# Phase 1 of a one-core transformer layer: the adaLN dot products in two passes, none on GpSimd, and the row modulation on ScalarE

## The chip, the cores and the metric

The kernel runs on one core of a Trainium2 chip as one launch. The metric is device time in microseconds (us) of that launch, the median of a few runs. The five engines of the core have one instruction queue each and run it in order: TensorE (PE in the profile; its weight loads are PEld), VectorE (DVE), ScalarE (ACT), GpSimd (POOL) and SyncE (SP). In this kernel SP issues every DMA transfer that the program asks for.

## The reference, cut to what matters

One layer for 2048 latent tokens and a prompt of 128 context tokens, both through the same weights, width 1024. Each of the two token kinds has its own conditioning vector: `c` for the latents, `c_ctx` for the prompt.

```python
def modulation(cond, w_ada, b_ada):
    m = jax.nn.silu(cond) @ w_ada + b_ada          # (1024) @ (1024, 6144)
    return jnp.split(m, 6, axis=-1)                # shift, scale, gate; twice
...
    u = rms_norm(x, g_pre) * (1.0 + scale) + shift
    p = u @ w_in                                   # q, k, v, B, C, x_in
```

Behind that come differential attention with a softmax over 2176 keys, a gated convolution, the output projection, and a SwiGLU feed-forward part with hidden width 2816; the second half of the layer is modulated in the same way by the remaining columns of `m`. Outputs are the two token sets and the keys and values of the prompt.

## The kernel before, in words

All matrix products of weights are made in split form: an operand is held as a high part `h` and a remainder `l` (`split`, L79: ScalarE copies to `h`, VectorE or GpSimd subtracts for `l`), and three matmuls replace one.

**Phase 1** (the stretch that the change touches) makes q, k and v of all tokens. Tokens go in nine groups: group 0 to 7 are 256 latent tokens each (two row tiles of 128), group 8 is the prompt (one tile). For a group, `norm_rows` (L193) loads rows `xt`, takes the sum of squares on ScalarE and scales by the reciprocal root on GpSimd; `u_part` (L211) transposes two of the eight 128-column blocks at a time on TensorE into the PSUM tile `up`, modulates them into `ut` (L223), splits them into `uh` and `ul`, and stores both in DRAM (`ud`) for later phases. `qkv_group` (L367) multiplies, rotates q and k, transposes them and stores them.

**The modulation** itself has no matmul. The host has cut `w_ada` into 48 blocks of 128 output columns, each transposed to 128x1024 (512 KB). Block b is loaded as `raw`, and the dot product of each of its rows with a conditioning vector, which lies in all partitions in `cb`, gives one column of `mc`: on VectorE one instruction with a sum (L138), on GpSimd a product `prod` (L142) that ScalarE then sums (L143). `ada_cols` (L145, instructions L148 to L150) makes shift and scale columns `modc` of that. Blocks 0 to 15 are shift and scale of the first half of the layer, blocks 2 kt and 2 kt + 1 those of column block kt; 16 to 31 are those of the second half; 32 to 47 are the gates.

**The start.** Group 0 runs along with the loading: for each kt from 0 to 7, `ada_first(kt)` loads two blocks and takes the dot products with both conditioning vectors (with `c` at raised priority), `qkv_weights(kt, (0, 1))` loads and splits the q and k weights of that kt (the remainders `wl` on GpSimd), and `follow` issues the twelve matmuls of that kt. The v weights follow (remainders on VectorE), then v of group 0. There are 6 `raw` buffers and 3 `rawq` buffers in the start, and 4 `raw` buffers later.

**Behind the start** the groups run in the order 0, 1, 2, 8, 3, 4, 5, 6, 7. While a group is multiplied, the rows and `u_part` of the next are made, and blocks 16 to 47 are worked off four per group (`ada_steps`), each with both dot products.

The order of instructions on each engine is not the order of the code alone: the build schedules them by a simulated timeline, with `tc.high_priority` raising some and `tc.issue_after` holding DMAs behind a named instruction. Phases 2 (attention, the convolution branch, output projection) and 3 (feed-forward) follow in the same launch.

Of the kernel before, what the change touches and what calls it, by code (L numbers as in the profile page):

```python
# [8 lines left out]
F32 = mybir.dt.float32  # L9
F32R = mybir.dt.float32r  # L10
BF16 = mybir.dt.bfloat16
AF = mybir.ActivationFunctionType
ALU = mybir.AluOpType
# [4 lines left out]
P = 128  # L18
D = 1024
# [13 lines left out]

POOLW = 960
WLV = (2,)
RAWS, FIRST = 6, "VG"
RATE = (670, 1500)


# [1 line left out]
def layer(ctx, tc, x_prompt, x_sample, cache_k, cache_v, cond, w_ada, b_ada, gcol,  # L41
# [81 lines left out]
    def cond_load(c):  # L123
        dma(cb[:, c, :], cond[c].partition_broadcast(P))
        S.activation(cb[:, c, :], cb[:, c, :], AF.Silu)

    first = {}

    def ada_load(b):
        raw = ad.tile([P, D], F32, tag="raw", name="raw", bufs=RAWS if b < 16 else 4)  # L130
        first[b] = dma(raw, w_ada[b])
        return raw

    def ada_sum(b, raw, c, eng):

        if eng is V:
            junk = cbp.tile([P, D], BF16, tag="jv", name="jv")
            V.scalar_tensor_tensor(junk, raw, 1.0, cb[:, c, :], op0=ALU.mult, op1=ALU.mult,  # L138
                                   accum_out=mc[:, b, c:c + 1])
        else:  # L140
            prod = cbp.tile([P, D], F32, tag="prod", name="prod", bufs=1)
            G.tensor_tensor(prod, raw, cb[:, c, :], op=ALU.mult)  # L142
            S.activation(prod, prod, AF.Copy, accum_out=mc[:, b, c:c + 1])  # L143

    def ada_cols(i, kt, cs):  # L145

# [3 lines left out]
        V.tensor_scalar(modc[:, i, cs, kt], modc[:, i, cs, kt], gc[:, i // 2, kt:kt + 1], None, op0=ALU.mult)  # L150

    def ada_first(kt):
        raws = [ada_load(2 * kt + j) for j in range(2)]
        with tc.high_priority(offset=400):
            for j in range(2):
                ada_sum(2 * kt + j, raws[j], 0, V)
            ada_cols(0, kt, slice(0, 1))
        if kt == 0:
            cond_load(1)
        for j in range(2):  # L160
            ada_sum(2 * kt + j, raws[j], 1, V if FIRST[j] == "V" else G)
        ada_cols(0, kt, slice(1, 2))

    def ada_later(b):
        raw = ada_load(b)
        ada_sum(b, raw, 0, V)
        ada_sum(b, raw, 1, V)
        if b < 32:
            if b % 2:
                ada_cols(2, (b - 16) // 2, slice(0, 2))  # L170
            return
        which, k = divmod(b - 32, KT)
        V.tensor_scalar(gates[:, which, :, k], mc[:, b, :], bc[:, b:b + 1], gc[:, 2 + which, k:k + 1],
                        op0=ALU.add, op1=ALU.mult)
        if b == 47:
            ps = psu.tile([P, 512], F32, tag="psu", name="gt")
            T.transpose(ps[:32, :P], gates.rearrange("p w c k -> p (w c k)"), ident)
            gt = p1.tile([32, P], F32, name="gt")
            S.copy(gt, ps[:32, :P])
            dma(ggd.rearrange("w (k n) -> (w k) n", n=P), gt)  # L180
# [29 lines left out]
    def u_part(xs, gi, kk, between=None):  # L210

        n, c = len(xs), int(gi == 8)
        w = n * P
        up = psu.tile([P, 512], F32, tag="psu", name="up")
        ut = p1.tile([P, 2, 256], F32, tag="ut", name="ut", bufs=2)
        h = p1.tile([P, 2, 256], F32R, tag="uh", name="uh", bufs=6)
        l = p1.tile([P, 2, 256], F32R, tag="ul", name="ul", bufs=6)
        for a in range(2):
            kt = 2 * kk + a
            for i in range(n):  # L220
                T.transpose(up[:, a * 256 + i * P:a * 256 + (i + 1) * P],
                            xs[i][:, kt * P:(kt + 1) * P], ident)
            V.tensor_scalar(ut[:, a, :w], up[:, a * 256:a * 256 + w],  # L223
                            modc[:, 0, c, kt:kt + 1], modc[:, 1, c, kt:kt + 1],
                            op0=ALU.mult, op1=ALU.add)
            if between:
                split(h[:, a, :w], l[:, a, :w], ut[:, a, :w])
                between(kt, h[:, a, :], l[:, a, :])
        if not between:
            split(h[:, :, :w], l[:, :, :w], ut[:, :, :w])  # L230
        dma(ud[gi][0, :, 2 * kk:2 * kk + 2, :w], h[:, :, :w])
        dma(ud[gi][1, :, 2 * kk:2 * kk + 2, :w], l[:, :, :w])
        return [(h[:, a, :], l[:, a, :]) for a in range(2)]
# [102 lines left out]
    for kk in range(4):  # L336
        u_part(xs, 0, kk, follow)
    behind.append(first[13])
    for kt in range(KT):
        qkv_weights(kt, (2,))  # L340
    x_ad.close()
# [91 lines left out]
            wb[m] = (h, l)  # L433

    order = [0, 1, 2, 8, 3, 4, 5, 6, 7]
    ada_work = list(range(16, 48))
    rows = {}
    for n, gi in enumerate(order):
        nxt = order[n + 1] if n < 8 else None

        def ada_steps(k):
            for b in ada_work[:k]:
                ada_later(b)
            del ada_work[:k]
# [6 lines left out]
        def part_step(a):  # L451
            if nxt is not None:
                u.setdefault(nxt, [])
                for kk in (0, 1) if a == 0 else (2, 3):
                    u[nxt] += u_part(rows[nxt], nxt, kk)
            ada_steps(1)

        steps = {1: rows_step, 0: lambda: part_step(0), 2: lambda: part_step(1)}
        if nxt is None:
# [424 lines left out]
    j = 0  # L884
# [275 lines left out]
```

## Time and profile before

| | |
|---|---|
| median of 3 runs | 3061.99 us (3058.2 to 3064.18) |
| the profiled execution's own time | 3067.98 us |
| its span, first to last instruction | 3066.2 us |
| busy in the span | PE 2909.8 us, DVE 1994.7 us, ACT 1444.4 us, POOL 1230.1 us |
| DMA | 525.25 MB, mean 171 GB/s |
| last matmul-like instruction of phase 1 on PE | starts at 406.6 us |
| first scores of phase 2 on PE | 406.72 us |

PE is busy nearly throughout, so the places to read are those where it is not: the first slices of the page's picture. A busy PE is not a PE at its peak there either, since its granted clock was below full speed in the first 125 us (0.70 in 25 to 50 us, 0.86 in 100 to 125 us).

### The profile page before, as it was taken

How to read it: one execution, taken by the hardware profiler on the slowest of the kernel's cores; microseconds unless marked ns; L12 is line 12 of the kernel's file. 1: busy time of each engine (PE TensorE's matmuls, PEld its weight loads, DVE VectorE, ACT ScalarE, POOL GpSimd, SP SyncE). 2: the span in 40 equal slices, each digit the busy share in tenths (PEclk: the TensorE clock that was granted, in tenths of full speed). 3: DMA queues.
4: the chain of work that ended last, by engine and by line, in shares of the span. 5: the costliest groups of instructions: out<-in, count | busy, mean ns of one | idle time of the engine just before them, and what ended most of it. 6: DMA issues, size and time to landing. Idle time of an engine off the chain costs nothing. (4 is left out here: it accounts for less than half of the span.)

```text
span 3066.2 us, 47162 instructions
## 1 busy us (share of the span) xinstructions
PE 2909.8 (95%) x16925; PEld 2653.8 (87%) x16925; DVE 1994.7 (65%) x3824; ACT 1444.4 (47%) x2651; POOL 1230.1 (40%) x1114
## 2 busy tenths in 40 slices
PE   4999989999999999999999999999999999999998
PEld 3778879999999999988889988999999998788886
DVE  7899568787787887863366765556655554554443
ACT  3323236565565565664445553544444443444442
POOL 7313125554545544532245654555444440111110
PEclk7999999999999999999999999999999999999999
DMA  7777564454454454457645565444633235766663
GB/s 250 244 251 247 171 198 129 137 173 123 138 168 128 132 159 124 114 162 224 196 140 152 154 200 195 150 147 153 227 136 101 96 103 199 238 220 218 220 220 118
DMA packets 351180, 525.25 MB, mean 171 GB/s; under 512 B 33089, under 2 KB 264673, under 8 KB 349153
## 3 DMA queue, kind: packets, MB, share of 16 engines
q1 hardware_dynamic: 350944, 522.23, 53.7%
q8 instruction: 133, 2.18, 0.3%
q14 instruction: 103, 0.84, 0.1%
HBM read 393.79 MB, written 128.34 MB: 170 GB/s over the span
## 5 line engine op out<-in xcount | busy, mean ns | idle before, releaser
L957 PE MATMUL psg<-u,wi 128*128 128x384 f32 (+1 forms) x1848 | 606.6, 331 | 28.4 <-ACT wi L81 11.6
L959 PE MATMUL psg<-u,wi 128*128 128x384 f32 (+1 forms) x1848 | 597.6, 329 | 9.8 <-DVE wi L82 9.8
L958 PE MATMUL psg<-u,wi 128*128 128x384 f32 (+1 forms) x1848 | 606.2, 328 | 0.0
L505 DVE TENSOR_SCALAR_CACHE_REDUCE e<-s 128x436 f32<-128x436 f32 (+2 forms) x648 | 373.4, 600 | 87.1 <-PE s L502 70.7
L957 PEld LDWEIGHTS psg<-u,wi 128*128 128x128 f32 x1848 | 349.6, 190 | 38.6 <-ACT wi L81 15.5
L959 PEld LDWEIGHTS psg<-u,wi 128*128 128x128 f32 x1848 | 348.1, 189 | 13.9 <-DVE wi L82 13.5
L502 PE MATMUL s<-km,qt 128*128 128x436 f32 (+1 forms) x1280 | 344.1, 372 | 13.2 <-DVE e L505 9.1
L82 DVE TENSOR_TENSOR wi<-st,wi 128x512 fp32r<-128x512 f32 x264 | 246.1, 935 | 160.8 <-ACT wi L81 157.0
L958 PEld LDWEIGHTS psg<-u,wi 128*128 128x128 f32 x1848 | 350.1, 189 | 0.3
L82 DVE TENSOR_TENSOR wo<-rawo,wo 128x1024 fp32r<-128x1024 f32 x132 | 167.0, 1265 | 252.3 <-ACT wo L81 252.3
L510 ACT ACTIVATE e<-e,nm 128x2176 f32<-128x2176 f32 (+1 forms) x136 | 273.9, 2014 | 78.2 <-DVE nm L509 77.3
L81 ACT CAST wi<-st 128x512 fp32r<-128x512 f32 x264 | 163.3, 619 | 279.6 <-PE psg L959 190.8
L1089 PE MATMUL psy<-wo,hhl 128*128 128x512 f32 x748 | 286.0, 391 | 1.8 <-DVE hhl L82 1.8
L1088 PE MATMUL psy<-wo,hhl 128*128 128x512 f32 x748 | 286.5, 390 | 0.9 <-DVE wo L82 0.9
L1087 PE MATMUL psy<-wo,hhl 128*128 128x512 f32 x748 | 286.2, 391 | 0.0
L81 ACT CAST wo<-rawo 128x1024 fp32r<-128x1024 f32 x132 | 139.1, 1054 | 294.3 <-PE psy L1089 284.1
L82 DVE TENSOR_TENSOR wi<-raw,wi 128x512 fp32r<-128x512 f32 x198 | 233.0, 1193 | 35.5 <-ACT wi L81 30.7
L502 PEld LDWEIGHTS s<-km,qt 128*128 128x128 f32 x1280 | 209.1, 190 | 26.1 <-DVE e L505 17.5
L81 ACT CAST ath<-t 128x512 fp32r<-128x512 f32 (+2 forms) x292 | 157.4, 555 | 114.9 <-PE t L546 107.6
L82 DVE TENSOR_TENSOR atl<-t,ath 128x512 fp32r<-128x512 f32 (+2 forms) x292 | 187.1, 649 | 36.4 <-ACT ath L81 35.7
L1060 POOL TENSOR_TENSOR rr<-rr,mhalf 128x1 f32<-128x1 f32 x17 | 13.1, 779 | 452.7 <-DVE rr L1059 452.7
L919 POOL TENSOR_TENSOR st<-raw,st 128x512 f32<-128x512 f32 x66 | 87.3, 1322 | 254.4 <-DVE wi L82 254.4
(264 smaller groups left out, 7040.5 us busy)
## 6 DMA issues: line engine op xcount, KB each, us to landing
raw<-in_w_fi SPq DMA_DIRECT2D x132, 512.0 KB, 4.2
rawo<-in_w_fo SPq DMA_DIRECT2D x132, 512.0 KB, 3.6
fu<-ud SPq DMA_DIRECT2D x256, 256.0 KB, 4.7
raw<-in_w_ada SPq DMA_DIRECT2D x48, 512.0 KB, 5.2
u2d<-hl SPq DMA_DIRECT2D x42, 512.0 KB, 3.9
u<-u2d SPq DMA_DIRECT2D x14, 1536.0 KB, 10.7
hr<-hid SPq DMA_DIRECT2D x110, 192.0 KB, 3.5
hid<-hid SPq DMA_DIRECT2D x88, 192.0 KB, 3.6
```

The source lines that it names most:

```text
L81: S.copy(h, src)
L82: (eng or V).tensor_tensor(l, src, h.bitcast(F32), op=ALU.subtract)
L502: mm = T.matmul(ps[:, :n], qt[:, s, m, t * P:(t + 1) * P], km[m][:, k0:k0 + n], start=(s == 0), stop=(s == 1))
L505: V.tensor_scalar(et[:, k0:k0 + n], ps[:, :n], SCALE, None, op0=ALU.mult, op1=ALU.max, accum_out=mx[:, ci:ci + 1])
L510: S.activation(et[:, :nk], et[:, :nk], AF.Exp, bias=nm, scale=1.0, accum_out=sm[:, t, m:m + 1])
L919: G.tensor_tensor(t, x, y, op=op)
L957: T.matmul(ps, h[:, ks], u[:, 0, kt, :n], start=start and kt == 0, stop=False, skip_group_check=not start)
L958: T.matmul(ps, h[:, ks], u[:, 1, kt, :n], start=False, stop=False, skip_group_check=not start)
L959: T.matmul(ps, l[:, ks], u[:, 0, kt, :n], start=False, stop=kt == 3, skip_group_check=not start)
L1087: T.matmul(banks[i][:, b, :], hh, woh_[:, bs], start=(f == 0), stop=False)
L1088: T.matmul(banks[i][:, b, :], hh, wol_[:, bs], start=False, stop=False)
L1089: T.matmul(banks[i][:, b, :], hl, woh_[:, bs], start=False, stop=(f == NF - 1))
```

## The change

Five edits, all in phase 1:

- `ada_first` takes only the dot products with `c`. Those of blocks 0 to 15 with `c_ctx` move into `ada_later`, which loads the block a second time: 16 more loads of 512 KB.
- All dot products are VectorE's; the GpSimd product and its ScalarE sum are gone (eight of each).
- `cb` of the prompt is loaded and passed through SiLU behind the start, not in its first step.
- `ut`, the modulation of the transposed rows, is one ScalarE instruction (scale and bias by column) where it was one of VectorE, 72 times.
- The prompt moves from the fourth place to the eighth: 0 to 6, 8, 7. The list of block work is 48 long (a late block of 0 to 15 beside one of 16 to 31, then 32 to 47) and is worked off six per group.

```diff
-RAWS, FIRST = 6, "VG"
+RAWS = 6
...
-    def ada_load(b):
-        raw = ad.tile([P, D], F32, tag="raw", name="raw", bufs=RAWS if b < 16 else 4)
+    def ada_load(b, early=True):
+        raw = ad.tile([P, D], F32, tag="raw", name="raw", bufs=RAWS if b < 16 and early else 4)
...
-    def ada_sum(b, raw, c, eng):
-
-        if eng is V:
-            junk = cbp.tile([P, D], BF16, tag="jv", name="jv")
-            V.scalar_tensor_tensor(junk, raw, 1.0, cb[:, c, :], op0=ALU.mult, op1=ALU.mult,
-                                   accum_out=mc[:, b, c:c + 1])
-        else:
-            prod = cbp.tile([P, D], F32, tag="prod", name="prod", bufs=1)
-            G.tensor_tensor(prod, raw, cb[:, c, :], op=ALU.mult)
-            S.activation(prod, prod, AF.Copy, accum_out=mc[:, b, c:c + 1])
+    def ada_sum(b, raw, c):
+
+        junk = cbp.tile([P, D], BF16, tag="jv", name="jv")
+        V.scalar_tensor_tensor(junk, raw, 1.0, cb[:, c, :], op0=ALU.mult, op1=ALU.mult, accum_out=mc[:, b, c:c + 1])
...
             for j in range(2):
-                ada_sum(2 * kt + j, raws[j], 0, V)
+                ada_sum(2 * kt + j, raws[j], 0)
             ada_cols(0, kt, slice(0, 1))
-        if kt == 0:
-            cond_load(1)
-        for j in range(2):
-            ada_sum(2 * kt + j, raws[j], 1, V if FIRST[j] == "V" else G)
-        ada_cols(0, kt, slice(1, 2))
 
     def ada_later(b):
+        if b < 16:
+            ada_sum(b, ada_load(b, False), 1)
+            if b % 2:
+                ada_cols(0, b // 2, slice(1, 2))
+            return
         raw = ada_load(b)
-        ada_sum(b, raw, 0, V)
-        ada_sum(b, raw, 1, V)
+        for c in range(2):
+            ada_sum(b, raw, c)
...
-            V.tensor_scalar(ut[:, a, :w], up[:, a * 256:a * 256 + w],
-                            modc[:, 0, c, kt:kt + 1], modc[:, 1, c, kt:kt + 1],
-                            op0=ALU.mult, op1=ALU.add)
+            S.activation(ut[:, a, :w], up[:, a * 256:a * 256 + w], AF.Identity, scale=modc[:, 0, c, kt:kt + 1],
+                         bias=modc[:, 1, c, kt:kt + 1])
...
     behind.append(first[13])
+    cond_load(1)
...
-    ada_work = list(range(16, 48))
+
+    order1 = [0, 1, 2, 3, 4, 5, 6, 8, 7]
+    ada_work = [b for k in range(16) for b in (k, 16 + k)] + list(range(32, 48))
...
-            ada_steps(1)
+            ada_steps(2)
```

The build's schedule moves with it. VectorE in the start before, between the modulation of one column block and that of the next (`jv` is the output of the dot product, `mc` its sum):

```order
L223 TENSOR_SCALAR ut<-up,modc 128x256
L138 SCALAR_TENSOR_TENSOR jv,mc<-raw,cb 128x1024
L82 TENSOR_TENSOR ul<-ut,uh 128x256
L149 TENSOR_SCALAR modc<-mc,bc 128x1
L138 SCALAR_TENSOR_TENSOR jv,mc<-raw,cb 128x1024
L150 TENSOR_SCALAR modc<-modc,gc 128x1
L138 SCALAR_TENSOR_TENSOR jv,mc<-raw,cb 128x1024
L148 TENSOR_SCALAR modc<-mc,bc 128x1
L223 TENSOR_SCALAR ut<-up,modc 128x256
```

and after the change, from one remainder `ul` to the next:

```order
L82 TENSOR_TENSOR ul<-ut,uh 128x256
L142 TENSOR_SCALAR modc<-mc,bc 128x1
L137 SCALAR_TENSOR_TENSOR jv,mc<-raw,cb 128x1024
L143 TENSOR_SCALAR modc<-mc,bc 128x1
L144 TENSOR_SCALAR modc<-modc,gc 128x1
L137 SCALAR_TENSOR_TENSOR jv,mc<-raw,cb 128x1024
L82 TENSOR_TENSOR ul<-ut,uh 128x256
```

Three dot products per column block became two, and `ut` is no longer in this queue. ScalarE in the start before:

```order
L81 CAST uh<-ut 128x256
L81 CAST wh_1_242<-rawq 128x512
L81 CAST wh_1_246<-rawq 128x512
L143 ACTIVATE prod,mc<-prod 128x1024
L81 CAST uh<-ut 128x256
L81 CAST wh_2_288<-rawq 128x512
```

and after:

```order
L81 CAST uh<-ut 128x256
L81 CAST wh_1_224<-rawq 128x512
L81 CAST wh_1_228<-rawq 128x512
L218 ACTIVATE ut<-up,modc 128x256
L81 CAST uh<-ut 128x256
L81 CAST wh_2_262<-rawq 128x512
```

In the place of the sum of `prod` stands the modulation, directly ahead of the split that needs it. SP's queue in the start, before (from the first block loads on):

```order
L74 DMA raw<-in_w_ada 128x1024 x2
L74 DMA cb<-in_cond 128x1024
L74 DMA xt<-in_x_sample 128x1024 x2
L74 DMA rawq<-in_w_qkv 128x1024
L74 DMA raw<-in_w_ada 128x1024 x2
L74 DMA rawq<-in_w_qkv 128x1024
L74 DMA raw<-in_w_ada 128x1024 x2
L74 DMA rawq<-in_w_qkv 128x1024
L74 DMA raw<-in_w_ada 128x1024 x2
L74 DMA rawq<-in_w_qkv 128x1024
L74 DMA raw<-in_w_ada 128x1024 x2
```

and after:

```order
L74 DMA raw<-in_w_ada 128x1024 x2
L74 DMA xt<-in_x_sample 128x1024 x2
L74 DMA rawq<-in_w_qkv 128x1024
L74 DMA raw<-in_w_ada 128x1024 x2
L74 DMA rawq<-in_w_qkv 128x1024
L74 DMA raw<-in_w_ada 128x1024 x2
L74 DMA rawq<-in_w_qkv 128x1024
L74 DMA raw<-in_w_ada 128x1024 x4
L74 DMA rawq<-in_w_qkv 128x1024
```

The rows come ahead of nothing but the first two blocks, and the second `cb` load stands further down, between block 13 and block 14. Behind the first few hundred instructions of phase 2 on each engine (about 490 on PE, 110 on VectorE), the rest of the program stands in the same order in both kernels.

More of the change, by code (lines that the diff above doesn't have):

```diff
@@ L435, in layer @@
     order = [0, 1, 2, 8, 3, 4, 5, 6, 7]
-    ada_work = list(range(16, 48))
+    order1 = [0, 1, 2, 3, 4, 5, 6, 8, 7]
+    ada_work = [b for k in range(16) for b in (k, 16 + k)] + list(range(32, 48))
     rows = {}
-    for n, gi in enumerate(order):
-        nxt = order[n + 1] if n < 8 else None
+    for n, gi in enumerate(order1):
+        nxt = order1[n + 1] if n < 8 else None
         def ada_steps(k):
```

## The prediction

> **What bounds the kernel now.** I read the busy shares first, then a table by stretch of time, then the waits of the engine that should be full, then groups and single rows in the stretch where it is not. The page, the times and the table of stretches (columns: stretch, its length, busy time and instructions of each engine, granted clock of PE, DMA share, GB/s):
>
> ```profile
> span 3066.2 us, 47162 instructions
> PE 2909.8 (95%) x16925; PEld 2653.8 (87%) x16925; DVE 1994.7 (65%) x3824; ACT 1444.4 (47%) x2651; POOL 1230.1 (40%) x1114
> ...
> 0.00:25.00 25.00, 5.81 (x16) 4.06 (x17) 11.81 (x26) 9.32 (x14) 13.91 (x14) 1.00 0.90 326
> 25.00:50.00 25.00, 13.48 (x36) 8.75 (x35) 25.00 (x40) 7.71 (x16) 22.29 (x11) 0.70 0.60 208
> 50.00:75.00 25.00, 17.70 (x50) 13.20 (x50) 24.13 (x46) 10.17 (x21) 18.55 (x11) 0.68 0.61 207
> 75.00:100.00 25.00, 20.78 (x88) 15.48 (x86) 18.97 (x40) 11.64 (x22) 11.96 (x9) 0.86 0.69 219
> ...
> 275.00:300.00 25.00, 25.00 (x131) 20.31 (x131) 22.32 (x40) 7.53 (x14) 5.40 (x3) 1.00 0.58 185
> ...
> 0.00:88.00 88.00, 45.86 (x128) 32.06 (x129) 70.19 (x130) 32.66 (x59) 65.58 (x41) 0.79 0.68 236
> 88.00:404.00 316.00, 305.77 (x1507) 244.74 (x1505) 247.82 (x474) 86.58 (x156) 80.99 (x55) 0.99 0.71 232
> ```
>
> PE is the bound of the whole at 95%, and what it loses in phase 1 it loses at the start: 88 − 45.9 = 42 us idle in the first 88 us, 316 − 305.8 = 10 us in the 316 us behind them. In the start VectorE is full (25.00 of 25, then 24.13), PE runs at a clock of 0.70 and less, and the transfers, which began at 326 GB/s, fall to 208. The start hands over to the steady stretch when v of group 0 is done, at 99.7 us:
>
> ```profile
> 86.90 1.10 PE L239 MATMUL pq<-wh,ul 128*128 128x512 f32 x4
> ...
> 99.29 0.41 PE L239 MATMUL pq<-wh,ul 128*128 128x512 f32 x1
> ```
>
> The first row ends the last column block of q and k of group 0 (88.0 us). What PE waits for (us, times, longest), in 0 to 88 us and then in 88 to 404 us:
>
> ```profile
> PE up L221 <- POOL xt L202: 20.1, 3, 16.8
> PE up L221 <- DVE ut L223: 18.3, 7, 4.9
> ...
> PE up L221 <- DVE ut L223: 3.2, 4, 1.7
> ```
>
> 16.8 us are the unavoidable first rows; the rest is mostly one wait per column block, for `ut`, which stands in VectorE's queue behind dot products. Why those are slow (groups in 15 to 88 us: count, busy, mean ns; then single rows):
>
> ```profile
> L138 DVE SCALAR_TENSOR_TENSOR jv<-raw,cb 128x1024 bf16<-128x1024 f32 x21 | 43.1, 2052 | 0.0
> L82 POOL TENSOR_TENSOR wl<-rawq,wh 128x512 fp32r<-128x512 f32 x16 | 28.2, 1780 | 9.2 <-ACT wh L81 9.2
> L142 POOL TENSOR_TENSOR prod<-raw,cb 128x1024 f32<-128x1024 f32 x7 | 21.6, 3079 | 0.0
> L223 DVE TENSOR_SCALAR ut<-up,modc 128x256 f32<-128x256 f32 x12 | 6.3, 532 | 4.0 <-PE up L221 4.0
> ...
> 7.97 1.22 DVE L138 SCALAR_TENSOR_TENSOR jv<-raw,cb 128x1024 bf16<-128x1024 f32 x1 [6.42 <-DMA raw<-in_w_ada]
> 44.91 3.10 DVE L138 SCALAR_TENSOR_TENSOR jv<-raw,cb 128x1024 bf16<-128x1024 f32 x1
> ...
> 43.61 3.32 POOL L142 TENSOR_TENSOR prod<-raw,cb 128x1024 f32<-128x1024 f32 x1
> ```
>
> A dot product takes 1.22 us with GpSimd idle and 3.10 us while GpSimd runs `prod`; the mean is 2.05 us. VectorE and GpSimd hold each other up, and the block buffers come free late, which is what slows the loads.
>
> **The change part by part.** *The start, work.* Of the start's 24 dot products on VectorE (three per column block) eight go: 8 × 2.05 = 16.4 us. The twelve `ut` go: 6.3 us. The 7 `prod` of the stretch go with their 21.6 us of GpSimd. The dot products left still meet `wl`; if they fall half way to 1.22, to 1.64, some 13 left in this stretch give 5 us. VectorE's 70.2 us become about 42, so it no longer sets the pace. ScalarE takes `ut` on. No 256-wide modulation on ScalarE is in the trace; the nearest rows are a 128-wide one with columns for scale and bias, and a plain copy of 256 from PSUM:
>
> ```profile
> L843 ACT ACTIVATE ur<-up,modc 128x128 f32<-128x128 f32 x40 | 16.4, 456 | 7.0 <-PE up L842 7.0
> L653 ACT COPY bt<-fb 128x256 f32<-128x256 f32 (+1 forms) x36 | 12.6, 362 | 30.0 <-PE fb L619 30.0
> ```
>
> Bounds 0.36 and 2 × 0.46 = 0.91 us; I take 0.55, the first row with a little for its longer tile. That is what VectorE took (0.53), so the chain from transpose to split keeps its length, and ScalarE, busy 32.7 us in 88, has room.
>
> *The start, transfers.* With the engines out of the way, bytes set the pace. The four rows of 25 us moved (326 + 208 + 207 + 219) × 25 = 24.0 MB up to the end of v of group 0, and the change takes none of that away, for the second load of the blocks stands behind it. At 326 GB/s 24.0 MB take 74 us; at 250, a rate like the 257 of the steady stretch quoted below, 96 us. I take 300, because queue order and buffers (three column blocks ahead) will leave some gaps: 80 us, a gain of 20 us (26 to 4 as bounds). The Trainium skill (SBUF — State Buffer, section "A bandwidth-pool intuition that's wrong") gives about 358 GB/s for HBM to one core and calls HBM the usual bottleneck; the trace agrees in so far as 326 GB/s came at a DMA share of 0.90. By that figure, an estimate, 24.0 MB take 67 us, the gain would be 33 us and the time 3027; no run here shows that rate held. The prompt's `cb` load leaves the first step, which brings the first rows forward by under 1 us; I count it within the 20.
>
> *Behind the start.* Here VectorE gets the 16 dot products back and loses 60 `ut`. The groups of 88 to 404 us, then 125 to 275 us by itself with the same two groups:
>
> ```profile
> L138 DVE SCALAR_TENSOR_TENSOR jv<-raw,cb 128x1024 bf16<-128x1024 f32 x64 | 83.8, 1310 | 0.1
> L223 DVE TENSOR_SCALAR ut<-up,modc 128x256 f32<-128x256 f32 (+1 forms) x60 | 30.0, 517 | 9.2 <-PE up L221 9.2
> ...
> 125.00:275.00 150.00, 144.55 (x712) 114.33 (x711) 142.13 (x278) 39.20 (x73) 43.75 (x28) 1.00 0.79 257
> L138 DVE SCALAR_TENSOR_TENSOR jv<-raw,cb 128x1024 bf16<-128x1024 f32 x55 | 71.1, 1292 | 0.1
> L223 DVE TENSOR_SCALAR ut<-up,modc 128x256 f32<-128x256 f32 (+1 forms) x25 | 12.0, 490 | 1.2 <-PE up L221 1.2
> ```
>
> 16 × 1.31 = 21.0 us come, 30.0 go: net −9 us of 247.8, with 68 us idle. Over the whole it costs nothing; the cover is that idle time. In 125 to 275 us it is thin: if all 16 fall there, 16 × 1.29 = 20.6 come, 12.0 go, and VectorE has 150 − 142.1 = 7.9 us idle, so 8.6 − 7.9 = 0.7 us too much, or some 9 us if none of that idle can be used. `ut` on ScalarE is 60 × 0.55 = 33 us on 86.6 of 316: covered. PE's wait for `ut` (3.2 us) may go. I take −2 us, bounds −10 (all of PE's idle) and +9.
>
> *The second load.* 16 blocks of 512 KB are 8.4 MB:
>
> ```profile
> raw<-in_w_ada SPq DMA_DIRECT2D x48, 512.0 KB, 5.2
> ```
>
> at 326 GB/s 26 us of transfer, beside a DMA share of 0.71 in 316 us, 92 us free: nothing. Without that cover it is 26 us. In SP's queue each stands ahead of stores of k, q and v; as it waits for a buffer that a dot product frees, those wait too, and their tiles (`sto`, two buffers; `vt`, one) are waited for by ScalarE. That is the third rival. *The prompt's place* changes no count; its products follow group 6 instead of group 2: 0. *Phases 2 and 3* keep their order: 0.
>
> The sum is −20 − 2 = −22 us. On the profiled execution (3068.0 by its own time, 6.0 above the median shown) that is 3046; on the median of 3062.0 it is **3040 us**.
>
> **The rivals.**
>
> 1. *The start runs at the full rate* and the last idle time goes too: −26 − 10 = −36, **3026 us**. For it: 326 GB/s is in the trace, with the first transfer's delay included. Against it: SP issues in order, and a load waits behind a store whose data is not ready.
> 2. *VectorE gives it back.* The dot products crowd the 150 us where VectorE is full, splits and rotations queue behind them, and PE waits: start −20, later +9, **3051 us**. For it: 142.1 of 150 busy. Against it: in that stretch PE idles 5.5 us only, though VectorE is full, so the dot products there are work that ran ahead.
> 3. *ScalarE's queue stalls the modulation* (slower). Ahead of `ut` now stand copies that wait for a store to free their tile (88 to 404 us: us, times, longest):
>
> ```profile
> ACT vt L81 <- DMA vd<-vt: 9.5, 5, 3.7
> ACT sto L253 <- DMA kpd<-sto: 8.2, 2, 6.4
> ACT sto L253 <- DMA kd<-sto: 5.1, 4, 2.5
> ACT sto L253 <- DMA qd<-sto: 3.7, 3, 3.1
> ```
>
>  26.5 us in all, which no `ut` waited behind before. With 8.4 MB more the free share of the DMA falls from 0.29 to about 0.29 − 26/316 = 0.21, and the waits grow by 0.29/0.21 to 37 us. If all of it reached PE the time would be 3062 − 20 + 37 = **3079 us**; it decides from 20 us of waits that reach PE on. Against it: each `up` has a second buffer and `ut` is made a group ahead. The Trainium skill (TensorE: Matmul & The Clock Gate, section "Architectural detail") says that ScalarE's queue is strictly first in, first out; the waits above agree with that but cannot show it.
> 4. *The start was not held by the engines.* If the 208 GB/s of 25 to 75 us come from SP's order and not from late buffers, the start keeps its 99.7 us: **3060 us**, −2 alone.
>
> **How the numbers follow.** The forecast has a chance of 0.52, the first rival 0.20, the second 0.16, the third 0.06, the fourth 0.06. About 0.2%, 6 us, is what a measurement of this kernel can tell from no change, so faster means below 3056: the forecast, the first, and most of the second rival, 0.86. The fourth and the rest of the second are no change, 0.08; slower 0.06. The forecast's own range is 3034 to 3048 (gain of the start 26 to 12, and 2 behind it). For 8 in 10 it takes in the first rival and most of the second: up to 3054, and down to 3018, 8 us below the first rival's time, since PE's 31 us of busy time at a clock of 0.69 in 25 to 75 us would be 21 us at full clock.
>
> **What would show it.** Right: v of group 0 ends on PE near 80 us instead of 99.7; 25 to 75 us show 280 GB/s or more and VectorE well under 25 of 25; dot products there have a mean near 1.6 us; no `prod`; `ut` on ScalarE takes 0.4 to 0.7 us; from there to the first scores as long as before, within 8 us. Wrong: the start ends later than 92 us with the DMA share still near 0.6 (fourth rival); PE idles over 20 us behind the start with ScalarE's `ut` as the releaser (third), or with VectorE's splits as the releaser (second).

## The result, and the profile after

| | before | after |
|---|---|---|
| median, measured side by side | 3063.09 us (3058.2 to 3066.7, 4 runs) | 3039.62 us (3038.8 to 3041.68, 4 runs) |
| span of the profiled execution | 3066.2 us | 3039.9 us |
| 96th / 144th matmul of q, k and v ends | 86.6 / 99.7 us | 62.1 / 81.9 us |
| first scores of phase 2 | 406.7 us | 384.3 us |

The ratio is 0.9923, interval 0.9911 to 0.9935: the changed kernel is 23 us faster, where 22 were forecast (3040 us). Group 0 takes 144 matmuls into `pq`, 96 of q and k and 48 of v. The times at which these counts are reached on PE are used below as milestones of the start; some of v's matmuls come before the last of q and k (88.0 us before), so the first count is near the end of q and k, not at it. The first scores are the milestone of phase 1. The page of the changed kernel, and its table by stretch (the columns are those of the table shown of before):

```profile
span 3039.9 us, 47168 instructions
PE 2902.1 (95%) x16925; PEld 2647.5 (87%) x16925; DVE 1961.1 (65%) x3768; ACT 1466.6 (48%) x2707; POOL 1204.6 (40%) x1106
...
0.00:25.00 25.00, 8.63 (x30) 6.38 (x31) 13.58 (x27) 9.90 (x16) 13.49 (x15) 1.00 0.93 345
25.00:50.00 25.00, 17.33 (x60) 11.28 (x58) 21.93 (x44) 10.31 (x21) 12.96 (x10) 0.86 0.97 372
50.00:75.00 25.00, 21.70 (x90) 16.16 (x90) 9.13 (x15) 17.16 (x34) 11.49 (x11) 0.86 0.77 246
75.00:100.00 25.00, 20.07 (x88) 15.31 (x89) 19.97 (x43) 14.16 (x27) 11.23 (x8) 0.86 0.86 308
```

In 25 to 50 us the transfers went from 208 to 372 GB/s at a DMA share of 0.97. In 50 to 75 us they fell to 246, and nothing in that row is full: VectorE is busy for 9.13 of 25, and PE comes nearest with 21.70. The row with which v of group 0 ends on PE, and the first scores of before and of after (instructions, then min/median/max duration in ns, first and last start):

```profile
81.27 0.63 PE L233 MATMUL pq<-wh,ul 128*128 128x512 f32 x1
```

```profile
L502 PE MATMUL s<-km,qt x33: 357/462/731, 406.7 to 419.8; 128*128 128x436 f32 x27, 128*128 128x432 f32 x6
```

```profile
L499 PE MATMUL s<-km,qt x58: 353/363/730, 384.3 to 419.1; 128*128 128x436 f32 x48, 128*128 128x432 f32 x10
```

So 99.7 − 81.9 = 17.8 us were gained in the start, and 22.4 − 17.8 = 4.6 us between it and the first scores. From there to the end of the span before took 2659.5 us and after 2655.6, though the code there is the same; what such a difference is worth is told with the last section. The groups of 15 to 88 us in the changed kernel, and what its PE waited for in 0 to 80 us:

```profile
L137 DVE SCALAR_TENSOR_TENSOR jv<-raw,cb 128x1024 bf16<-128x1024 f32 x15 | 23.7, 1581 | 1.2 <-DMA raw<-in_w_ada 1.2
L82 POOL TENSOR_TENSOR wl<-rawq,wh 128x512 fp32r<-128x512 f32 x16 | 26.1, 1662 | 8.6 <-ACT wh L81 8.6
L218 ACT ACTIVATE ut<-up,modc 128x256 f32<-128x256 f32 x23 | 12.6, 561 | 28.8 <-DVE modc L144 15.6 <-PE up L216 10.7 <-DVE ul L82 2.5
```

```profile
PE up L216 <- POOL xt L197: 17.4, 3, 13.8
PE up L216 <- ACT ut L218: 6.2, 5, 2.3
```

The dot product came down from 2.05 to 1.58 us, `ut` on ScalarE takes 0.56 us, and PE waits 6.2 us for it (the same up to 88 us), where it waited 18.3 up to 88 us before.

### The profile page after: what moved, and what is told of

It reads as the page before. It is cut to its first block, busy times and chain, and to the rows that moved or that the text cites. A ratio compares the mean times of both kernels' runs of the same rounds, so it can differ in the third digit from the quotient of the medians.

```text
span 3039.9 us, 47168 instructions
## 1 busy us (share of the span) xinstructions
PE 2902.1 (95%) x16925; PEld 2647.5 (87%) x16925; DVE 1961.1 (65%) x3768; ACT 1466.6 (48%) x2707; POOL 1204.6 (40%) x1106
## 4 chain that ended last, share of the span: by engine, by line
PE 63%; DVE 12%; DMA 10%; issue 8%; POOL 4%; ACT 3%; SPq 0%; DVEq 0%; POOLq 0%; ACTq 0%
PE s L499 7%; PE psg L956 6%; PE psg L954 6%; PE psg L955 6%; PE psy L1086 5%; PE psy L1085 5%; PE psy L1084 5%; PE t L543 3%; DMA u2d<-hl 3%; DVE jv L137 2%; DVE wi L82 2%; PE psx L722 2%; PE psx L723 2%; PE psx L721 2%; PE o L536 2%
## 5 line engine op out<-in xcount | busy, mean ns | idle before, releaser
L499 PEld LDWEIGHTS s<-km,qt 128*128 128x128 f32 x1280 | 210.6, 192 | 23.3 <-DVE e L502 14.1
```

What stands on the lines that cost most here:

```text
L499: mm = T.matmul(ps[:, :n], qt[:, s, m, t * P:(t + 1) * P], km[m][:, k0:k0 + n], start=(s == 0), stop=(s == 1))
```

## The experiments

The theory of the prediction: GpSimd's product and VectorE's dot products hold each other up, this keeps block buffers and loads late, and without it bytes set the pace of the start. Against it stood that one of the other edits (`ut` on ScalarE, the second pass, the prompt's place) brings the gain, or that the start is still held by engines. Each kernel is measured beside before; the second number is the ratio to it with its interval.

| kernel | median us | ratio to before | 96th / 144th matmul, us | first scores, us |
|---|---|---|---|---|
| before_no_prod | 3043.19 | 0.9944 [0.9929, 0.9959] | 75.0 / 87.8 | 400.6 |
| before_ut_scalar | 3055.15 | 0.9982 [0.9973, 0.9992] | 85.4 / 98.4 | 403.3 |
| one_load | 3038.61 | 0.9919 [0.9904, 0.9934] | 74.2 / 87.5 | 389.0 |
| after | 3039.62 | 0.9923 [0.9911, 0.9935] | 62.1 / 81.9 | 384.3 |
| ut_vector | 3038.26 | 0.9915 [0.9896, 0.9935] | 61.9 / 80.1 | 384.2 |
| third_load | 3037.22 | 0.9923 [0.9908, 0.9937] | 59.9 / 76.4 | 388.3 |
| prompt_4th | 3037.44 | 0.9919 [0.9900, 0.9937] | 59.7 / 77.3 | 382.8 |
| dots_twice | 3055.86 | 0.9976 [0.9963, 0.9988] | 73.5 / 87.6 | 398.0 |
| half_bytes | 3032.55 | 0.9894 [0.9878, 0.9910] | 56.8 / 77.4 | 377.7 |
| wl_vector | 3030.61 | 0.9904 [0.9889, 0.9918] | 58.8 / 76.9 | 376.8 |
| rawq4 | 3029.42 | 0.9904 [0.9874, 0.9933] | 58.4 / 70.8 | 376.8 |
| wl_rawq4 | 3031.93 | 0.9897 [0.9882, 0.9912] | 58.5 / 70.8 | 376.9 |
| wl_all | 3022.48 | 0.9867 [0.9852, 0.9882] | 55.2 / 72.8 | 374.4 |

How fine these are: after, third_load and prompt_4th have the same order of instructions in the start (on PE for the whole of group 0, in SP's queue up to 64 us), and their 144th matmul ends at 81.9, 76.4 and 77.3 us. About 5 us at that milestone, and about 5 us in a total, are no finding by themselves. The starts of the other kernels are each scheduled anew by the build, so an edit moves other instructions too: the transfers in SP's queue in before_no_prod, for example, have the order of before only for the first 20, up to 26 us.

### One part of the change alone

**before_no_prod**: the kernel before, with all dot products on VectorE.

```diff
-RAWS, FIRST = 6, "VG"
+RAWS, FIRST = 6, "VV"
```

> The kernel before with one edit: all dot products on VectorE (no product on GpSimd, no sum of it on ScalarE); both conditioning vectors from one load, ut on VectorE, the prompt fourth. Theory D (GpSimd's product is the cost: while it runs, VectorE's dot products take up to 3.1 us for 1.2): 32 dot products at about 1.6 us take VectorE 51 us where 24 took 49, and GpSimd loses 25 us of work; v of group 0 ends at 88 to 94 us (99.7 before, 87.5 with one load and ut on ScalarE) and the time is 3039 to 3048 us. Theory E (it takes the second pass, or ut off VectorE, to gain): v of group 0 ends at 95 us or later, time 3052 us or more.

Its table by stretch, and then its dot products in 15 to 88 us:

```profile
25.00:50.00 25.00, 13.35 (x49) 8.99 (x47) 25.00 (x44) 6.43 (x13) 16.33 (x11) 0.86 0.75 251
50.00:75.00 25.00, 17.07 (x55) 12.47 (x56) 25.00 (x54) 6.43 (x13) 10.07 (x7) 0.80 0.52 185
```

```profile
L138 DVE SCALAR_TENSOR_TENSOR jv<-raw,cb 128x1024 bf16<-128x1024 f32 x28 | 46.7, 1667 | 1.0 <-DMA raw<-in_w_ada 1.0
```

VectorE has eight dot products more to do, is full in both rows, and the start still ends 11.9 us earlier (87.8 against 99.7), because one takes 1.67 us and not 2.05. 28 dot products now take 46.7 us where 21 took 43.1. ScalarE, too, had waited for the products. In 15 to 88 us of before:

```profile
ACT prod L143 <- POOL prod L142: 13.0, 5, 6.2
```

That wait is gone as well, but VectorE was not kept idle by it (25.00 and 24.13 of 25 in 25 to 75 us of before), so it was VectorE's time that held the start there. This is the experiment that carries the first step of the prediction: what GpSimd's product cost was not its own time but VectorE's.

The total falls by 18 us, but of these only 6.1 are there at the first scores. Part of the 11.9 us is lost at once, since PE waits 6.6 us for `ut` of the next group, which stands in VectorE's queue; the 145th matmul ends at 96.2 us, where it ended at 102.7. The other 12 us of the total lie in phases 2 and 3, whose code is the same (last section).

**before_ut_scalar**: the kernel before, with `ut` on ScalarE alone; **one_load**: with both, so that only the second pass, the late `cb` load and the prompt's place are missing from the change.

```diff
-            V.tensor_scalar(ut[:, a, :w], up[:, a * 256:a * 256 + w],
-                            modc[:, 0, c, kt:kt + 1], modc[:, 1, c, kt:kt + 1],
-                            op0=ALU.mult, op1=ALU.add)
+            S.activation(ut[:, a, :w], up[:, a * 256:a * 256 + w], AF.Identity, scale=modc[:, 0, c, kt:kt + 1],
+                         bias=modc[:, 1, c, kt:kt + 1])
```

> The kernel before with one edit: ut on ScalarE; half of the prompt's dot products stay on GpSimd in the start. Theory D: the dot products still meet GpSimd's products; only ut's own 6 us leave VectorE, and ut waits for the columns that the slow dot products make: v of group 0 ends at 93 to 99 us, time 3053 to 3063 us. Theory B (the queue ahead of ut was the cost): v of group 0 ends at 85 us or earlier, time 3045 us or less.

> The kernel before with ut on ScalarE and all dot products on VectorE, but both conditioning vectors still taken from the one load in the start, the prompt in its fourth place, no second load. Theory A: VectorE has 32 dot products in the start instead of 16, some 16 x 1.6 = 26 us more than in the changed kernel, and paces it again: v of group 0 ends at 88 to 95 us; behind the start 16 dot products and 8.4 MB fewer save at most 2 us; time 3044 to 3053 us. Theory B: v of group 0 ends at 80 to 84 us and the time is 3036 to 3042 us, the second load is not needed.

Groups of before_ut_scalar in 15 to 88 us:

```profile
L138 DVE SCALAR_TENSOR_TENSOR jv<-raw,cb 128x1024 bf16<-128x1024 f32 x21 | 45.6, 2169 | 0.0
L142 POOL TENSOR_TENSOR prod<-raw,cb 128x1024 f32<-128x1024 f32 x7 | 18.0, 2575 | 5.3 <-ACT prod L143 5.3
```

With `prod` still there, the dot products take 2.17 us, and freeing VectorE of `ut` is worth 1.3 us in the start, within what these milestones can tell, and 0.2% in all. With `prod` gone (one_load beside before_no_prod) it changes nothing in the start (87.5 and 87.8) but brings the first scores from 400.6 to 389.0; what it is worth there lies behind the start, and the totals (0.9944 and 0.9919, with intervals that overlap) hardly show it. one_load met neither of its two theories whole: its start ends at 87.5, as expected if VectorE paces it, and its total is 3038.6 all the same, that of the change. In the changed kernel it is gone:

**ut_vector**: the changed kernel with `ut` back on VectorE (the diff above, turned round).

> The changed kernel with one edit undone: the modulation ut is VectorE's again (72 instructions of about 0.52 us); the two passes of dot products, no product on GpSimd and the prompt's late place stay. Theory A (the start is paced by its transfers once VectorE and GpSimd have less to do): VectorE gets about 7 us more in the start, of which it has some 30 idle, so v of group 0 ends at 82 to 85 us (81.7 in the changed kernel); behind it VectorE has 30 us more on its 316, some of it in the stretch where it is full: 0 to 5 us. Time 3040 to 3047 us. Theory B (the gain is the shorter wait for ut, which no longer stands behind dot products): v of group 0 ends at 90 us or later, time 3050 us or more.

3038.26 us and the first scores at 384.2: the same as the change; the start (80.1 us) and the total are a little below what either theory expected. Of the five edits this one is worth nothing once the others are made. But that holds only beside the second pass. With GpSimd's product gone, `ut` on ScalarE alone moves the first scores by 11.6 us (400.6 to 389.0), the second pass, the late `cb` load and the prompt's place without it by 16.4 (400.6 to 384.2), and all together by 16.3: the two relieve the same engine, and the gains do not add. **third_load**: the changed kernel with one more load of each of the blocks 0 to 15 behind the start, which nothing reads.

```diff
         if b < 16:
+            ada_load(b, False)
             ada_sum(b, ada_load(b, False), 1)
```

> The changed kernel with blocks 0 to 15 loaded once more behind the start (16 loads of 512 KB that nothing reads). If the transfers behind the start have the room that I claimed (share 0.74 in 100 to 375 us), the first scores come at 384 to 388 us and the time is 3038 to 3044 us. If the second load already costs, one more costs as much again: first scores at 392 us or later, time 3048 us or more.

8.4 MB more cost 4 us at the first scores and nothing that can be told in the total. The change's own second load is of the same size. **prompt_4th**: the prompt back at its place, the blocks in the order of their numbers.

```diff
-    order1 = [0, 1, 2, 3, 4, 5, 6, 8, 7]
-    ada_work = [b for k in range(16) for b in (k, 16 + k)] + list(range(32, 48))
+    order1 = [0, 1, 2, 8, 3, 4, 5, 6, 7]
+    ada_work = list(range(48))
```

> The changed kernel with the prompt back at the fourth place and the list of block work in the order of its numbers (so that the second pass over blocks 0 to 15 is done before the prompt is modulated); four of the five edits stay. Prediction's step: the place changes no count and costs nothing: v of group 0 ends at 79 to 82 us, the first scores come at 380 to 388 us (384.3), the total is 3034 to 3044. Rival: with the prompt early, the second pass crowds VectorE in the 150 us where it is full, and PE waits there: the first scores come at 390 us or later, the total is 3046 or more.

First scores at 382.8 against 384.3: the place is worth nothing, and the second pass can be done early in the stretch without harm.

So the chain before, before_no_prod, one_load, after adds one part at a time and ends the start at 99.7, 87.8, 87.5 and 81.9 us and phase 1 at 406.7, 400.6, 389.0 and 384.3 us. In the totals (3063, 3043, 3039, 3040) the last step does not show.

### What the changed start waits for

**dots_twice**: the changed kernel with every early dot product made twice (16 more).

```diff
                 ada_sum(2 * kt + j, raws[j], 0)
+                ada_sum(2 * kt + j, raws[j], 0)
```

> The changed kernel with each of the start's 16 dot products made twice: 16 x 1.2 to 1.9 us = 20 to 30 us more on VectorE, no byte more. Theory A (VectorE is covered by the transfers in the changed start): v of group 0 ends at most 6 us later, time 3039 to 3046 us. Theory C' (VectorE still paces the start): it ends 20 us or more later, time 3058 to 3070 us.

Its table by stretch, and the wait of PE for `ut` in 0 to 100 us:

```profile
25.00:50.00 25.00, 15.01 (x42) 10.25 (x42) 24.82 (x37) 6.84 (x14) 15.11 (x9) 0.73 0.84 270
50.00:75.00 25.00, 16.65 (x60) 11.82 (x60) 22.64 (x43) 11.75 (x24) 14.30 (x9) 0.86 0.54 193
```

```profile
PE up L217 <- ACT ut L219: 16.1, 8, 4.0
```

About 24 us of VectorE's time cost 11 us at the 96th matmul, 6 at the end of v, 14 at the first scores and 16 in the total (the profiled execution, 3046.5, is the fastest of six). The end of v is as the first theory expected, the total is 10 us above its range: what the start hides is paid behind it. VectorE in the changed start (21.93 of 25 in 25 to 50 us) is not far from being the bound again. **half_bytes**: the changed kernel with only the first half of each early block loaded and read twice, so that the first modulation of the latents is not the reference's and 4.2 MB are left out of the start.

```diff
+        if b < 16 and early:
+            first[b] = dma(raw[:, :512], w_ada[b][:, :512])
+            return raw[:, :512].unsqueeze(1).to_broadcast([P, 2, 512])
...
-        V.scalar_tensor_tensor(junk, raw, 1.0, cb[:, c, :], op0=ALU.mult, op1=ALU.mult, accum_out=mc[:, b, c:c + 1])
+        j_, c_ = junk, cb[:, c, :]
+        if len(raw.shape) == 3:
+            j_, c_ = junk.rearrange("p (x d) -> p x d", x=2), c_.rearrange("p (x d) -> p x d", x=2)
+        V.scalar_tensor_tensor(j_, raw, 1.0, c_, op0=ALU.mult, op1=ALU.mult, accum_out=mc[:, b, c:c + 1])
```

> The changed kernel, but in the start only half of each block of w_ada is loaded and read twice by the dot product, so VectorE works as long and 4.2 MB of 24 are not moved; the latent tokens' first modulation is then not the reference's. Theory A (transfers pace the start): at 300 GB/s 14 us less if nothing else takes over, at least 5: v of group 0 ends at 68 to 77 us, time 3026 to 3035 us. Theory C (the chain of engines or SP's queue paces the changed start): v of group 0 ends at 79 to 82 us, time 3037 to 3041 us.

```profile
25.00:50.00 25.00, 17.42 (x62) 11.47 (x63) 22.18 (x45) 13.73 (x27) 15.97 (x11) 0.91 0.90 296
50.00:75.00 25.00, 20.45 (x86) 15.52 (x85) 8.42 (x16) 15.55 (x32) 12.34 (x13) 0.89 0.77 231
```

At the 300 GB/s of the prediction 4.2 MB are 14 us. The start ended 4.5 us earlier, which is no more than that milestone can tell, and the first scores came 6.5 us earlier. In 25 to 50 us the DMA share fell from 0.97 to 0.90 and the 96th matmul came 5.3 us earlier, so up to about 50 us the transfers were near their limit, though they were not alone in setting the pace. The second row stays at 231 GB/s with bytes to spare: behind 50 us it was something else. What SP's queue, which issues the loads, waited for in 50 to 82 us of the changed kernel:

```profile
SPq L74 <- ACT uh L81: 8.4, 4, 4.9
SPq L74 <- POOL wl L82: 5.6, 2, 3.7
```

`wl` is GpSimd's remainder of the q and k weights, 1.66 us each, and frees a `rawq` buffer; `uh` is a store that stands in the queue ahead of loads. **wl_vector** has the remainders of q and v on VectorE (`WLV` lists the parts whose remainders VectorE makes), **wl_all** those of q, k and v:

```diff
-WLV = (2,)
+WLV = (0, 2)
```

```diff
-WLV = (2,)
+WLV = (0, 1, 2)
```

**rawq4** has a fourth buffer, and **wl_rawq4** has it together with the first of these edits:

```diff
-        raw = ad.tile([P, 2, 512], F32, tag="rawq", name="rawq", bufs=3)
+        raw = ad.tile([P, 2, 512], F32, tag="rawq", name="rawq", bufs=4)
```

> The changed kernel with half of the q and k weights' remainders in the start on VectorE instead of GpSimd (8 instructions, 0.68 us there, 1.3 to 2.3 us on GpSimd). If SP's waits for those remainders (10 us in the first 80 us) hold the later loads of the start back: v of group 0 ends at 76 to 79 us, time 3034 to 3038 us. If the start is held by the transfers until 50 us and by PE and ScalarE's queue behind that: no change, 80 to 83 us and 3037 to 3043 us.

> The changed kernel with all remainders wl of the q, k and v weights on VectorE: GpSimd has only the rows' scaling in the start. Theory 1: what GpSimd does on 512-wide tiles costs twice (its own 1.65 us, and VectorE's stretched dot products), and VectorE needs 0.8 us for one: the dot products of 15 to 88 us fall from a mean of 1.58 to 1.3 us or less, v of group 0 ends at 76 us or before, the total is 3026 to 3033, as with two thirds of the remainders on VectorE (3030.6) or a little less. Theory 2: VectorE, in order, becomes the engine that the first column blocks wait for: 25 to 50 us show it at 24 of 25 or more, v of group 0 ends at 79 us or later, the total is 3036 to 3045.

> The changed kernel with four buffers for the q, k and v weights as they are loaded (rawq) where it has three; nothing else. Theory 1: in 50 to 75 us of the changed kernel SyncE waits for GpSimd's remainders wl to free rawq, and this holds the loads; a fourth buffer takes that wait away: 50 to 75 us show 290 GB/s or more where they showed 246, v of group 0 ends at 77 us or before (80.6), the total is 3032 to 3038. Theory 2: the waits for rawq follow from late matmuls and splits, and more depth only lets loads wait later: v of group 0 ends at 79 to 82 us, the total is that of the changed kernel, 3036 to 3043.

> The remainders wl of q and v on VectorE, those of k on GpSimd, and four rawq buffers: the two edits together. If each takes away a different wait, v of group 0 ends at 74 us or before (76.5 with the remainders alone) and the first scores come at 374 us or before (376.8), total 3024 to 3031. If both take away the same wait, v ends at 76 to 78 us, the first scores come at 375 to 379, total 3027 to 3035.

wl_all in the table by stretch, and its groups in 15 to 88 us:

```profile
25.00:50.00 25.00, 19.48 (x81) 14.01 (x80) 21.56 (x53) 13.64 (x27) 4.04 (x4) 0.96 1.03 397
50.00:75.00 25.00, 21.83 (x89) 16.54 (x89) 14.16 (x26) 18.11 (x35) 7.49 (x8) 0.84 0.83 261
```

```profile
L137 DVE SCALAR_TENSOR_TENSOR jv<-raw,cb 128x1024 bf16<-128x1024 f32 x17 | 22.5, 1324 | 0.0
L82 DVE TENSOR_TENSOR wl<-rawq,wh 128x512 fp32r<-128x512 f32 x23 | 16.4, 728 | 7.8 <-ACT wh L81 7.7
```

All 16 remainders of GpSimd went to VectorE, and VectorE is busy for 21.56 us of 25 to 50 us, where it was 21.93: a remainder takes 0.73 us there, 12 us for 16, and shorter instructions gave back most of it, by an estimate 4 us in 16 dot products (1.32 us for 1.58) and 4 in the 8 small splits of `ut` (0.42 for 0.92 on average). The 96th matmul ends 6.9 us earlier, v of group 0 9.1, the first scores 9.9:

```profile
L499 PE MATMUL s<-km,qt x70: 353/362/734, 374.4 to 419.1; 128*128 128x436 f32 x56, 128*128 128x432 f32 x14
```

**wl_all has the lowest median: 3022.48 us (3020.39 to 3025.27), ratio 0.9867 to before.** The intervals of it and of after do not touch (that of rawq4 reaches into it); one ratio over the other is 0.994. Of the 17 us between the two medians 10 are at the first scores; the other 7 lie in phases 2 and 3, whose code is the same, and are not explained here by anything but the spread described below.

The fourth buffer alone brought v to 70.8 us, as expected if the wait for `rawq` held the loads, but 50 to 75 us show 251 GB/s and not the 290 expected. None of the three edits raised that stretch by much (wl_vector 236, wl_all 261, where the changed kernel has 246), so it is not settled what holds it; all three moved more in 25 to 50 us (396, 397 and 391 GB/s for wl_vector, wl_all and rawq4, for 372). With both edits (wl_rawq4) v ends at 70.8 as well, and the first scores at 376.9, as with each alone. So all three end phase 1 at the same time, and the two edits do not add: the gain of 6 us that the fourth buffer has at the end of v over wl_vector is lost by the first scores. In wl_rawq4 it is lost at the hand-over: VectorE, in the order of its queue, waits 4.0 us up to 73.2 us for a load of other data (`lt`), PE then waits 3.8 us for `ut`, and the 145th matmul ends at 78.3 us, in wl_vector at 78.7. In rawq4 it ends at 75.3, and where the rest goes these runs do not show. The total of rawq4 (3021.82 to 3042.83) is too wide to rank.

## Why the prediction was right, step by step

**What bounds the kernel: right, and shown for the start.** VectorE and GpSimd hold each other up. before_no_prod takes GpSimd's product away, gives VectorE more to do, and gains 12 us in the start and 6 at the first scores.

**The start, work.** The dot product was set at 1.64 us and came at 1.58; `ut` on ScalarE was set at 0.55 and came at 0.56. Up to the end of v VectorE was busy for 70.2 + 9.4 = 79.6 us before and 37.9 + 10.6 = 48.5 after, 31 us less, where 16.4 + 6.3 + 5 = 27.7 were summed. The rows behind that, beside the one of 0 to 88 us shown of before, are its next stretch and two of the changed kernel:

```profile
88.00:99.70 11.70, 11.70 (x60) 9.42 (x58) 9.42 (x18) 5.88 (x10) 1.12 (x1) 1.00 0.86 267
```

```profile
0.00:62.00 62.00, 35.94 (x121) 24.80 (x122) 37.94 (x76) 29.57 (x55) 37.65 (x34) 0.89 0.88 327
62.00:82.00 20.00, 16.29 (x73) 12.11 (x71) 10.56 (x19) 13.23 (x26) 5.73 (x6) 0.85 0.78 241
```

What did not hold is the sentence behind the sum, that VectorE no longer sets the pace: dots_twice shows some 24 us of it costing 6 at the end of v and 14 at the first scores, so it was partly covered, not free. And the 6.3 us of `ut` were counted as a part of the gain; ut_vector shows that they are worth nothing there. The sum has no term for PE's own time, and it moved too: by the rows for the start PE was busy for 57.6 us up to the end of v before and for 52.2 after, with nearly the same matmuls and a granted clock of 0.86 where it was 0.70 and 0.68 in 25 to 75 us. So about 5 of the 17.8 us are PE's busy time and about 12 its idle time.

**The start, transfers: the number right, the reason right for half of it.** 327 × 62 + 241 × 20 = 25.1 MB in 82 us are 306 GB/s; 300 was taken, 17.8 us were gained and 20 forecast; third_load and prompt_4th, with the same start, gained 23.3 and 22.4, so 17.8 and 20 cannot be told apart. That the mean came out at 306 is in part luck, as it is of two halves. Up to 50 us the DMA share is 0.93 and 0.97; behind it 0.77, and there bytes are not the limit: half_bytes saves 4.5 us of the 14 that pure bytes would give, and wl_all ends v 9 us earlier with the same bytes. The forecast sign, 280 GB/s or more in 25 to 75 us, holds for the mean (309) and fails for its second half (246). The first rival (3026, the start at the full rate) is not what the change did; wl_all, which also takes the remainders off GpSimd, came near its time (3022.5).

**The late `cb` load: mis-sized.** The prediction gave it under 1 us, and called the 16.8 us that PE waits for the first rows unavoidable. With the load behind the start that wait is 13.8 us; in before_no_prod, which loads `cb` early but has no product on GpSimd, it is 16.1. So some 2 us of the start's gain go with the rows' place ahead of that load; no run moves this load alone.

**Behind the start: within the bounds, and too small to tell.** It was −4.6 us against −2, within −10 to +9. But from the end of v to the first scores prompt_4th takes 305.5 us and ut_vector 304.1, where after takes 302.4 and before 307.0; so the sign is not shown, and neither is the reason given, since `ut` is back on VectorE in ut_vector. PE idles 302.2 − 293.0 = 9.2 us there, before 307.0 − 295.0 = 12.0, by these rows of the changed kernel and of before:

```profile
82.00:384.20 302.20, 292.98 (x1451) 233.84 (x1449) 239.25 (x456) 100.74 (x193) 78.53 (x49) 1.00 0.76 258
```

```profile
99.70:406.70 307.00, 294.96 (x1457) 236.07 (x1456) 239.62 (x459) 81.29 (x148) 79.87 (x54) 0.99 0.71 231
```

The second rival (VectorE gives 9 us back there) fell with it.

**The second load and the prompt's place: nothing**, as put, by third_load and prompt_4th; up to 4 us at the first scores cannot be excluded for the load.

**The third rival (ScalarE's queue)** had its cause right and its price wrong. ScalarE's waits for stores, in 100 to 384 us of before and then of after:

```profile
ACT sto L253 <- DMA kpd<-sto: 8.2, 2, 6.4
ACT vt L81 <- DMA vd<-vt: 6.7, 4, 3.7
ACT sto L253 <- DMA kd<-sto: 5.1, 4, 2.5
ACT sto L253 <- DMA qd<-sto: 3.7, 3, 3.1
```

```profile
ACT vt L81 <- DMA vd<-vt: 22.3, 6, 6.7
ACT sto L247 <- DMA kd<-sto: 17.7, 10, 6.4
ACT sto L247 <- DMA qd<-sto: 14.5, 4, 6.8
```

They grew from 23.7 to 54.5 us, more than the growth to 37 that the rival reckoned with, and PE's idle time fell: `up` has its second buffer and `ut` is a group ahead, which was the argument against it. It can be seen in small at the end of the start, where `ut` stands in ScalarE's queue behind a sum of squares that waited 3.2 us for its rows. PE, then ScalarE:

```profile
76.02 0.60 PE L216 MATMUL up<-ident,xt 128*128 128x128 f32 x2 [2.30 <-ACT ut L218]
78.03 0.69 PE L216 MATMUL up<-ident,xt 128*128 128x128 f32 x2 [1.41 <-ACT ut L218]
```

```profile
74.37 1.06 ACT L195 ACTIVATE junk<-xt 128x1024 bf16<-128x1024 f32 x1 [3.20 <-DMA xt<-in_x_sample]
75.33 0.19 ACT L195 ACTIVATION_READ_ACCUMULATOR junk<-xt 128x1 f32 x1
75.42 0.55 ACT L218 ACTIVATE ut<-up,modc 128x256 f32<-128x256 f32 x1
```

3.7 us of PE are lost there. In third_load and prompt_4th, with the same order, the sum of squares did not wait for its rows, and PE lost 1.3 and 0.8 us: this is a part of the spread of that milestone.

**The fourth rival** (the start keeps its 99.7 us, because SP's order holds it) fell with the result, 81.9. But SP's order had a share in the slow loads. What its queue waited for in 25 to 75 us of before:

```profile
SPq L74 <- ACT uh L81: 15.8, 3, 11.5
SPq L74 <- DVE modc L150: 14.4, 4, 7.9
```

The second row is the wait that the prediction meant, for dot products that free a `raw` buffer (`modc` follows them). The first is for stores of `uh` that stand in the queue ahead of loads. In the same stretch of the changed kernel the waits for `uh` are 7.1 us and those for dot products 4.1 (`modc` 2.3, `jv` 1.8). The build reordered the queue with the edits, so the runs do not separate the two.

## What to carry to other kernels

When an engine is full, ask first what stretches its instructions: here the largest gain in the start came not from taking work off VectorE but from taking GpSimd's two-operand work away from beside it, even where VectorE had to do that work itself. Check whether the edits of one change are each worth something by undoing them one at a time: the prompt's place was worth nothing here, and `ut` nothing beside the second pass, though it gained 11.6 us at the first scores without it. And when a rate is forecast as a mean, look at its parts: a start that is held by bytes in one half and by something else in the other gains little from fewer bytes.

## What the runs showed that was not expected

**The remainders on GpSimd stretch the small splits too, not only the dot products.** GpSimd and then VectorE in the changed kernel:

```profile
16.53 11.77 POOL L82 TENSOR_TENSOR wl<-rawq,wh 128x512 fp32r<-128x512 f32 x6
33.05 6.20 POOL L82 TENSOR_TENSOR wl<-rawq,wh 128x512 fp32r<-128x512 f32 x4 [4.75 <-ACT wh L81]
```

```profile
31.40 1.21 DVE L137 SCALAR_TENSOR_TENSOR jv<-raw,cb 128x1024 bf16<-128x1024 f32 x1
...
32.54 0.42 DVE L82 TENSOR_TENSOR ul<-ut,uh 128x256 fp32r<-128x256 f32 x1
...
34.43 1.45 DVE L82 TENSOR_TENSOR ul<-ut,uh 128x256 fp32r<-128x256 f32 x1 [1.10 <-ACT uh L81]
35.80 2.31 DVE L137 SCALAR_TENSOR_TENSOR jv<-raw,cb 128x1024 bf16<-128x1024 f32 x1
```

From 28.3 to 33.05 us GpSimd stands still, and the dot product takes 1.21 us and `ul` 0.42. Beside four `wl` in a row they take 2.31 and 1.45: about 1.0 to 1.1 us more for the short one and the long one alike. In the first 90 us of the changed kernel five dot products ran beside `wl` for 60% of their time or more, and ten beside none: 2.01 and 1.22 us on average. For `ul` it is 1.22 (five) and 0.42 (three). The addition is 0.8 us for both, so here the cost goes by the instruction and not by its length. `ut` on VectorE, which reads one tile from PSUM, took 0.53 us in before beside GpSimd's work as without it. The Trainium skill (SBUF — State Buffer, section "🔬 SBUF: two separate sides") has VectorE's instructions with two SBUF inputs and GpSimd's take a shared port in turn, the later one waiting for the whole of the other. An equal addition for unequal lengths agrees with that. In the prediction only the dot product's stretch was priced.

**The loads can exceed 358 GB/s.** 372 GB/s in 25 us of the changed kernel, 397 in wl_all at a DMA share of 1.03 (all bytes moved, the few stores included). The prediction weighed a figure of 358 as the most that could be held. The Trainium skill (Perfetto Trace Analysis, section "Roofline") says that a core alone may go beyond that share; the rows agree for 25 us; in the 25 us behind, the two kernels fell to 246 and 261 GB/s.

**The clock dips at scattered places in phases 2 and 3.** Two of the twelve stretches of 25 us behind 375 us in which the changed kernel's granted clock was below 0.96 (the last stretch, where PE is nearly idle, is not counted):

```profile
600.00:625.00 25.00, 23.05 (x146) 21.91 (x145) 17.80 (x53) 15.04 (x28) 13.56 (x20) 0.93 0.71 225
...
2600.00:2625.00 25.00, 22.33 (x85) 17.59 (x85) 17.67 (x18) 11.45 (x18) 10.52 (x6) 0.86 0.83 269
```

wl_all has seven such stretches, most at other places. From the first scores to the end of the span the profiled executions took 2659.5 us (before), 2655.6 (after), 2655.9 (ut_vector), 2644.4 (wl_all) and 2640.7 (before_no_prod), with the same code there. So phase 1's own milestones say more of a change to phase 1 than the total does. The dips are not the whole of it: busy time of PE times the missing share of the clock, added up over 400 to 3025 us, is an estimated 23 us in before and 14 in before_no_prod, about half of the 19 us between these two, and PE is idle there for 91 and 77 us. What sets the dips off, and what the idle time, was not tried.
